# Ten dense blocks, a branch moved ahead, and two tokens per half block in the last layer of a transformer stack

## The chip, the cores and the metric

The program runs on one core of one Trainium2 chip. The metric is its device time in microseconds (us), the median of several runs. One execution is also taken by the hardware profiler, and all rows below come from that one. TensorE is written PE (matmuls) and PEld (weight loads), VectorE DVE, ScalarE ACT, GpSimd POOL, and SyncE, which issues most of the transfers, SP.

## The reference

A stack of two attention layers and a mixer layer over 256 tokens of width 2048 in float32 ends with a feed-forward layer of 16,384 experts, and this last layer is where the change lies. Its weights w_u and w_v have one row of 2048 numbers for each expert. Every token picks 8 x 16 experts through two sets of 128 sub-keys:

```
q  = (h @ w_pq).reshape(T, 8, 2, 128)
s1 = einsum('thd,kd->thk', q[:, :, 0], sub_keys_1);  s2 = the same with q[:, :, 1], sub_keys_2
v1, i1 = top_k(s1, 16);  v2, i2 = top_k(s2, 16)
cand = v1[..., :, None] + v2[..., None, :]           # 16 x 16 for each head
sc, ci = top_k(cand, 16)
e1 = i1[ci // 16];  e2 = i2[ci % 16];  experts = e1 * 128 + e2
gates = softmax(sc)
a = <h_t, w_u[expert]> for each pick;  c = gates * gelu(a)
y_t = sum over picks of c * w_v[expert]
x = rmsnorm(x + y) * g_final
```

## The kernel before, in words

The first 1,530 us are the three layers in front, and the change does not touch them. The rest is the function `peer` (L1283). It does not gather w_u: it multiplies all of it with all tokens, in 128 blocks (one for each e2) of 128 experts (e1), each block in two halves of eight 128 x 128 tiles. Numbers of float32 are split in a hi and a lo part, so one half block is 8 matmuls of hi with the hi and lo parts of the activations (512 columns) and 8 of lo with the hi parts (256 columns). ScalarE makes hi (`wh`, L1464), VectorE lo (`wl`, L1468), two buffers each; the raw weights (`wr`, 512 KB a half block) have four buffers. The result goes through a gelu into the tile C[e1, e2, token].

Beside these half blocks three other things pass, written into them by `between` (L1596), in the written order of PE, ACT and DVE:

- The top-k, on VectorE, as a generator of small steps with weights (`topk_steps`, L1373). Each half block takes steps until their weights sum to 14.
- The picks. When top-k is done (and two short finishing generators), VectorE and ScalarE build one-hot rows for each token (`pair_ops`, L1510), and in the next half block TensorE turns them into the token's gate matrix with four small bfloat16 matmuls (`pair_mms`, L1524). Tokens go by pairs, spread so that the 128th pair is made by half block 194 (`q_end`): most half blocks take two tokens, every sixth or seventh takes four. Every four tokens one multiplication on VectorE (L1537) puts the gates into C.
- When all tokens are through, `places` (L1541) counts which experts are used by the first 128 tokens only, by both halves, by the second only, and by none, and gives each expert row of C a place in that order. `send` (L1580) writes 128 rows of C, 1088 bytes each, to their places in the DRAM tensor `cd`, with one indirect DMA on POOL's queue for each e2. The last ND blocks of e2 are left out: they are dense, all their experts are taken in place from C.

After the w_u blocks comes w_v. `product` (L1658) adds one block's coefficients (256 tokens) times 1024 columns of w_v into eight PSUM banks: 12 matmuls for both token halves, 6 for one. The dense blocks load their w_v rows as they lie (L1706). The others are packed (`packed`, L1726): SP loads 128 packed rows of cd (`cb`, 136 KB), which must wait for all the sends; POOL gathers the 128 w_v rows that they name (`vb`, 1 MB, seven buffers); ScalarE and VectorE split them; TensorE multiplies. `FIRST` and `SECOND` say which packed blocks are multiplied for the first token half and which for the second; blocks behind both are skipped. Should a count overrun these cuts, a flag (`more`, L1572) opens a spare path behind a branch (`tc.If`, L1760) that multiplies what was left out; each engine reads the flag and branches by itself.

Order: in the w_u part PE, ACT and DVE follow the written order. In the w_v part the planner orders all engines by its own model of the time. Instructions on either side of a branch can't be exchanged. The last two packed blocks are fetched and split ahead of the branch and multiplied behind it, bank by bank, with the final norm.

Of the kernel before, what the change touches and what calls it, by code (L numbers as in the profile page):

```python
# [12 lines left out]
BF = mybir.dt.bfloat16  # L13
# [1256 lines left out]
    peer(nc, tc, io, xd1, hT, rbc, hp, sp, W, ident, mm, raw_block, split_block, proj_T, blocks, power_rstd, new_pair)  # L1270


ND = 4
NC = 128 - ND

CROW = 272


FIRST = (0, 76)
SECOND = (26, 103)  # L1280


def peer(nc, tc, io, xd, hT, rbc, hp, sp, W, ident, mm, raw_block, split_block, proj_T, blocks, power_rstd, new_pair):  # L1283
    cd = io["cd"]
    with ExitStack() as es:
# [35 lines left out]
        with ExitStack() as pu_stack:  # L1321
# [185 lines left out]

            bank4 = [None]

            def pair_ops(p):  # L1510

                ws = []
                for t in (2 * p, 2 * p + 1):
                    w = pk.tile([128, 5, 128], BF, name="oh", bufs=4)
                    nc.vector.tensor_scalar(w[:, 4, :], iob, eT[:, 1, t:t + 1], None, op0=OP.is_equal)  # L1515
                    nc.vector.tensor_scalar(w[:, 0, :], iob, eT[:, 0, t:t + 1], None, op0=OP.is_equal)
                    nc.vector.tensor_scalar(w[:, 1, :], iob, eT[:, 1, t:t + 1], gP[:, 0, t:t + 1],
                                            op0=OP.is_equal, op1=OP.mult)
                    for a in (1, 2):
                        nc.scalar.activation(w[:, 1 + a, :], w[:, 4, :], AF.Copy, scale=gP[:, a, t:t + 1])  # L1520
                    ws.append(w)
                return ws

            def pair_mms(p, ws):  # L1524
                if p % 2 == 0:
                    bank4[0] = pq.tile([128, 4, 128], F32, name="pq")
                for i, w in enumerate(ws):
                    t = 2 * p + i
                    for a in range(3):
                        mm(bank4[0][:, t % 4, :], w[:, 0, :], w[:, 1 + a, :], t % 4 == 0 and a == 0, t % 4 == 3 and a == 2)  # L1530
                    mm(cnt[:, t // 128, :], w[:, 0, :], w[:, 4, :], t == 0, t == 255)
                return bank4[0]

            def quad_end(q4, bank, n):
# [54 lines left out]
            steps = topk_steps()  # L1589
            topk_done = False  # L1590
            left = 0
            pair, waiting = 0, []
            placing = q_from = None
            q_end = 2 * 97

            def between(i, low):  # L1596


                nonlocal pair, q4, q_from, left, topk_done, placing
                if not topk_done or fins:  # L1600
                    low()
                    if fins and next(fins[0], "end") == "end":
                        fins.pop(0)
                        if topk_done:

                            nc.vector.tensor_scalar(C[:, :, 256:257].bitcast(I32).rearrange("p a o -> p (a o)"), iob,
                                                    128.0, row, op0=OP.mult, op1=OP.add)
                    left += 14
                    while left > 0 and not topk_done:
                        w = next(steps, None)  # L1610
                        topk_done = w is None
                        left -= w or 0
                    return
                full, ws = [], list(waiting)
                waiting.clear()
                if pair < 128 and q_from is None:
                    q_from = i
                for p, w in ws:
                    b4 = pair_mms(p, w)
                    if p % 2:  # L1620
                        full.append((p // 2, b4))
                while pair < 128 and pair * (q_end - q_from) < 128 * (i + 1 - q_from):
                    waiting.append((pair, pair_ops(pair)))
                    pair += 1
                low()
                if placing and next(placing, "end") == "end":
                    placing = False
                for p, b4 in full:
                    quad_end(p, b4, done[0])
                    q4 += 1  # L1630
                    if q4 == 64:
                        placing = places()
                        next(placing)

            pu_stack.enter_context(tc.manual_schedule(engines={mybir.EngineType.PE, mybir.EngineType.Activation, mybir.EngineType.DVE}))
            split_next(0)()
            for e2 in range(128):
                u_block(e2)
# [19 lines left out]
        def product(c2, b, hi, lo, tbs, first=False, off=0):  # L1658
            for tb in tbs:
                t = slice(tb * 128 - off, (tb + 1) * 128 - off)  # L1660
                for j in range(2):
                    o = py[tb][2 * b + j]
                    w = slice(j * 512, (j + 1) * 512)
                    mm(o, c2[:, 0, t], hi[:, w], first, False)
                    mm(o, c2[:, 1, t], hi[:, w], False, False)
            for tb in tbs:
                t = slice(tb * 128 - off, (tb + 1) * 128 - off)
                for j in range(2):
                    mm(py[tb][2 * b + j], c2[:, 0, t], lo[:, j * 512:(j + 1) * 512], False, False)
# [3 lines left out]
        def split_half(v, b, into=None):  # L1673

            src = v[:, b * 1024:(b + 1) * 1024]
            i = turn[0]
            turn[0] += into is None
            hi = into[0] if into else hp.tile([128, 1024], F32R, name="hT")
            nc.scalar.activation(hi, src, AF.Copy)  # L1679
            if into:  # L1680
                lo = into[1]
            elif i % 3 < 2:
                lo = W["pool"].tile([128, 1024], F32R, name="wr", bufs=W["raw"])
            else:
                lo = W["pool"].tile([128, 1024], F32R, name="wl", bufs=W["lo"])
            nc.vector.tensor_tensor(lo, src, hi.bitcast(F32), op=OP.subtract)  # L1686
            return hi, lo
# [11 lines left out]
        two = []  # L1699

        more_reg = nc.values_load(flag[0:1, 0:1], min_val=0, max_val=1)
        for i, e2 in enumerate(range(NC, 128)):
            c2 = c_place()
            halves(c2, C[:, e2, :256])
            for b in range(2):
                hi, lo = split_block(io["w_v"][e2 * 128:(e2 + 1) * 128, b * 1024:(b + 1) * 1024])  # L1706
                product(c2, b, hi, lo, (0, 1), first=i == 0)
# [5 lines left out]
        def fetch(j, tbs, into=None):  # L1713
            c = vp.tile([128, CROW], F32, name="cb", bufs=8)
            nc.sync.dma_start(c, cd[j * 128:(j + 1) * 128, :])
            v = vp.tile([128, 2048], F32, name="vb", bufs=7)
            nc.gpsimd.indirect_dma_start(v, None, wide, bass.IndirectOffsetOnAxis(c[:, 256:257].bitcast(I32), 0))  # L1717
            c2, off = into or c_place(), 0
            if len(tbs) == 2:
                halves(c2, c[:, :256])  # L1720
            else:
                off = 128 * tbs[0]
                halves(c2[:, :, :128], c[:, off:off + 128])
            return c2, v, off

        def packed(j, tbs):  # L1726
            c2, v, off = fetch(j, tbs)
            for b in range(2):
                hi, lo = split_half(v, b)
                product(c2, b, hi, lo, tbs, off=off)  # L1730
            return v

        def halves_of(j):
            return tuple(tb for tb, (a, z) in enumerate((FIRST, SECOND)) if a <= j < z)

        one = [j for j in range(NC) if len(halves_of(j)) == 1]
        both = [j for j in range(NC) if len(halves_of(j)) == 2]
        last_js, both = both[-2:], both[:-2]
        order, both = both[:4], both[4:]
        late = [xd[:, 0, :], xd[:, 1, :], io["g_final"].to_broadcast([128, D])]  # L1740
        while one or both:
            if one and len(one) >= len(both):
                order.append(one.pop(0))
            else:
                order.append(both.pop(0))
        xg = [vp.tile([128, D], F32, name=f"xg{i}") for i in range(3)]
        for i, j in enumerate(order):
            v = packed(j, halves_of(j))
            if i >= len(order) - 12 and i % 2 == 0 and late:

                k = 3 - len(late)
                nc.gpsimd.tensor_copy(xg[k][:, :1], v[:, :1])
                nc.sync.dma_start(xg[k], late.pop(0))

        last = []
        for i, j in enumerate(last_js):
            c2, v, _ = fetch(j, (0, 1), vp.tile([128, 2, 256], F32R, name="lc", bufs=2))
            last.append((c2, [split_half(v, b, [vp.tile([128, 1024], F32R, name="lw", bufs=8) for _ in range(2)])
                              for b in range(2)]))
        with tc.If(more_reg, preferred_fallthrough_block=False):  # L1760
            for r in range(NC):
                tbs = tuple(tb for tb in range(2) if tb not in halves_of(r))
                if tbs:
                    packed(r, tbs)
        g = xg[2].rearrange("p (c n) -> p c n", c=4)
        rs = []
        for tb in range(2):
# [126 lines left out]
```

## Time and profile before

| | before |
|---|---|
| median of 3 runs | 2858.99 us (2858.84 to 2860.04) |
| the profiled execution | 2855.46 us |
| its span | 2853.7 us |
| PE, PEld busy | 2757.1 us (97%), 2289.3 us (80%) |
| DVE, ACT, POOL busy | 1910.4 us (67%), 1583.8 us (56%), 725.9 us (25%) |
| mean TensorE clock granted | 0.987 of full |

A busy share is an average over stages with different limits, so the table alone does not say what a change in one stage is worth. The page also has the span in forty slices of 71 us:

```
PE   8999999999999999989999999999999993999998
DVE  7545576656767555565566998888887662766665
```

Each digit is the busy share of a slice in tenths, 9 being 90% or more.

### The profile page before, as it was taken

Reading aid. Unit: us, or ns where it says so; the run is one execution under the profiler, and the core shown is the slowest. Engines: PE = TensorE matmul, PEld = TensorE weight load, DVE = VectorE, ACT = ScalarE, POOL = GpSimd, SP = SyncE. Lnnn points to the kernel's source line nnn. Section 1 sums busy time; section 2 is a strip of 40 time slices with the busy share of each in tenths; the row PEclk is TensorE's granted clock in tenths of the full one; section 3 lists DMA queues with packets and bytes.
Section 4 is the critical chain, followed back from the end, with each engine's and each line's share of the span. In section 5 each row is a group of like instructions: output and inputs, shape, how many; then the busy total and the mean of one; then the engine's idle time right before and its main releaser. Section 6 shows DMA issues by size and latency. Waiting matters only on the chain. (4 is left out here: it accounts for less than half of the span.)

```text
span 2853.7 us, 41401 instructions
## 1 busy us (share of the span) xinstructions
PE 2757.1 (97%) x14566; PEld 2289.3 (80%) x14566; DVE 1910.4 (67%) x3525; ACT 1583.8 (56%) x2943; POOL 725.9 (25%) x669
## 2 busy tenths in 40 slices
PE   8999999999999999989999999999999993999998
PEld 5877778887788888878888888888888882888886
DVE  7545576656767555565566998888887662766665
ACT  4445565545565544444454455888775442655554
POOL 6312320103121000020001232212223885322330
PEclk9999999999999999999999999999999996999999
DMA  6566443665445655566565555444445885988883
GB/s 229 174 220 196 135 141 119 208 191 172 155 129 163 229 199 167 180 214 224 167 202 178 181 186 182 147 149 147 148 145 178 265 263 226 343 290 298 282 323 126
DMA packets 158810, 561.74 MB, mean 197 GB/s; under 512 B 19584, under 2 KB 33536, under 8 KB 145024
## 3 DMA queue, kind: packets, MB, share of 16 engines
q1 hardware_dynamic: 137808, 433.71, 47.4%
q0 software_dynamic: 20784, 125.29, 11.7%
q8 instruction: 117, 1.92, 0.3%
q14 instruction: 101, 0.83, 0.1%
HBM read 531.17 MB, written 27.75 MB: 196 GB/s over the span
## 5 line engine op out<-in xcount | busy, mean ns | idle before, releaser
L204 DVE TENSOR_TENSOR wl<-wr,wh 128x1024 fp32r<-128x1024 f32 (+1 forms) x467 | 598.7, 1284 | 469.8 <-ACT wh L202 399.3
L202 ACT ACTIVATE wh<-wr 128x1024 fp32r<-128x1024 f32 (+1 forms) x467 | 492.9, 1056 | 588.6 <-PE pp L187 500.4
L187 PE MATMUL pp<-hT,wh 128*128 128x512 f32 x2880 | 736.8, 398 | 0.0
L187 PE MATMUL pp<-wh,hT 128*128 128x512 f32 x2688 | 697.0, 400 | 5.6 <-ACT wh L202 3.7
L187 PEld LDWEIGHTS pp<-wh,hT 128*128 128x128 f32 x2688 | 502.2, 190 | 128.6 <-ACT wh L202 8.5
L187 PEld LDWEIGHTS pp<-hT,wh 128*128 128x128 f32 x2880 | 517.1, 189 | 94.4 <-issue 0.3
L187 PEld LDWEIGHTS pp<-hT,wl 128*128 128x128 f32 x2880 | 393.0, 190 | 29.3 <-DVE wl L204 0.7
L187 PE MATMUL pp<-hT,wl 128*128 128x256 f32 x2880 | 403.0, 283 | 0.3 <-DVE wl L204 0.3
L187 PE MATMUL pp<-wl,hT 128*128 128x512 f32 x1344 | 373.9, 400 | 10.7 <-DVE wl L204 10.7
L1468 DVE TENSOR_TENSOR wl<-wr,wh 128x1024 fp32r<-128x1024 f32 x256 | 315.1, 1231 | 19.7 <-ACT wh L1464 17.7
L187 PEld LDWEIGHTS pp<-wl,hT 128*128 128x128 f32 x1344 | 248.3, 189 | 68.9 <-DVE wl L204 13.8
L1464 ACT ACTIVATE wh<-wr 128x1024 fp32r<-128x1024 f32 x256 | 269.9, 1054 | 39.8 <-PE pp L187 23.3
L1679 ACT ACTIVATE hT<-vb 128x1024 fp32r<-128x1024 f32 x202 | 210.8, 1059 | 127.9 <-PE py L187 98.1
L1686 DVE TENSOR_TENSOR wr<-vb,hT 128x1024 fp32r<-128x1024 f32 x135 | 165.4, 1229 | 66.8 <-PE py L187 53.5
L1717 POOL DMA_INDIRECT vb<-w_v,cb x103 | 127.2, 1234 | 269.0 <-ACT hT L1679 97.4
L1584 POOL DMA_INDIRECT cd<-C,posi x124 | 168.1, 1356 | 50.4 <-issue 31.7
L1520 ACT ACTIVATE oh<-oh,gP 128x128 bf16<-128x128 bf16 x512 | 166.8, 391 | 20.1 <-DVE oh L1515 19.8
L187 PE MATMUL py<-hT,c 128*128 128x512 f32 x600 | 152.6, 389 | 0.0
L187 PE MATMUL py<-hT 128*128 128x512 f32 x592 | 150.4, 389 | 0.0
L187 PEld LDWEIGHTS py<-hT,c 128*128 128x128 f32 x600 | 112.6, 188 | 23.3
L187 PEld LDWEIGHTS py<-hT 128*128 128x128 f32 x592 | 111.1, 188 | 23.0
L1686 DVE TENSOR_TENSOR wl<-vb,hT 128x1024 fp32r<-128x1024 f32 x67 | 82.2, 1228 | 33.5 <-PE py L187 27.1
(444 smaller groups left out, 3055.7 us busy)
## 6 DMA issues: line engine op xcount, KB each, us to landing
wr<-w_u SPq DMA_DIRECT2D x256, 512.0 KB
wr<-w_even SPq DMA_DIRECT2D x104, 512.0 KB
wr<-w_out SPq DMA_DIRECT2D x96, 512.0 KB
wr<-w_odd SPq DMA_DIRECT2D x96, 512.0 KB
wr<-w_in SPq DMA_DIRECT2D x64, 512.0 KB
wr<-w_mem SPq DMA_DIRECT2D x32, 512.0 KB
wr<-w_pq SPq DMA_DIRECT2D x32, 512.0 KB
cb<-cd SPq DMA_DIRECT2D x103, 136.0 KB
```

Source lines behind the costliest of these rows:

```text
L187: nc.tensor.matmul(out, lhsT=lhsT, rhs=rhs, start=start, stop=stop, skip_group_check=True)
L202: nc.scalar.activation(hi, raw, AF.Copy)
L204: (lo_eng or nc.vector).tensor_tensor(lo, raw, hi.bitcast(F32), op=OP.subtract)
L1464: nc.scalar.activation(hi, raw, AF.Copy)
L1468: nc.vector.tensor_tensor(lo, raw, hi.bitcast(F32), op=OP.subtract)
L1520: nc.scalar.activation(w[:, 1 + a, :], w[:, 4, :], AF.Copy, scale=gP[:, a, t:t + 1])
L1584: i = nc.gpsimd.indirect_dma_start(cd, bass.IndirectOffsetOnAxis(posi[:, e2:e2 + 1], 0), src, None).ins
L1679: nc.scalar.activation(hi, src, AF.Copy)
L1686: nc.vector.tensor_tensor(lo, src, hi.bitcast(F32), op=OP.subtract)
L1717: nc.gpsimd.indirect_dma_start(v, None, wide, bass.IndirectOffsetOnAxis(c[:, 256:257].bitcast(I32), 0))
```

## The change

Ten blocks are dense instead of four, so 118 instead of 124 are sent and packed, and the cuts follow. Top-k steps are taken by 16 units instead of 14. From the half block in which the picks begin, each takes exactly two tokens. The dense blocks and the fetch and split of the first two packed blocks (both token halves) stand in a region in which PE, ACT, DVE and SP follow the written order. Behind it stands the branch, and behind the branch the products of these two blocks and all other packed blocks. The last two blocks are fetched in the same way as before, without a branch behind them.

```diff
-ND = 4
+ND = 10
 NC = 128 - ND
-FIRST = (0, 76)
-SECOND = (26, 103)
+FIRST = (0, 73)
+SECOND = (25, 99)
...
-            def pair_ops(p):
-                ws = []
-                for t in (2 * p, 2 * p + 1):
-                    w = pk.tile([128, 5, 128], BF, name="oh", bufs=4)
...
+            def token_ops(t):
+                w = pk.tile([128, 5, 128], BF, name="oh", bufs=4)
...
-            q_end = 2 * 97
...
-                    left += 14
+                    left += 16
...
-                while pair < 128 and pair * (q_end - q_from) < 128 * (i + 1 - q_from):
-                    waiting.append((pair, pair_ops(pair)))
-                    pair += 1
+                while tok < min(256, 2 * (i + 1 - q_from)):
+                    waiting.append((tok, token_ops(tok)))
+                    tok += 1
...
         more_reg = nc.values_load(flag[0:1, 0:1], min_val=0, max_val=1)
+        e = mybir.EngineType
+        head = ExitStack()
+        head.enter_context(tc.manual_schedule(engines={e.PE, e.Activation, e.DVE, e.SP}))
         for i, e2 in enumerate(range(NC, 128)):
...
-        last_js, both = both[-2:], both[:-2]
-        order, both = both[:4], both[4:]
+        first_js, order, last_js, both = both[:2], both[2:4], both[-2:], both[4:-2]
...
-        for i, j in enumerate(order):
-            v = packed(j, halves_of(j))
...
-        last = []
-        for i, j in enumerate(last_js):
-            c2, v, _ = fetch(j, (0, 1), vp.tile([128, 2, 256], F32R, name="lc", bufs=2))
-            last.append((c2, [split_half(v, b, [vp.tile([128, 1024], F32R, name="lw", bufs=8) for _ in range(2)])
-                              for b in range(2)]))
+        def ahead(js):
+            out = []
+            for j in js:
+                c2, v, _ = fetch(j, (0, 1), vp.tile([128, 2, 256], F32R, name="lc", bufs=2))
+                out.append((c2, [split_half(v, b, [vp.tile([128, 1024], F32R, name="lw", bufs=8) for _ in range(2)])
+                                 for b in range(2)]))
+            return out
+        first = ahead(first_js)
+        head.close()
         with tc.If(more_reg, preferred_fallthrough_block=False):
             for r in range(NC):
                 tbs = tuple(tb for tb in range(2) if tb not in halves_of(r))
                 if tbs:
                     packed(r, tbs)
+        for c2, ws in first:
+            for b in range(2):
+                product(c2, b, *ws[b], (0, 1))
+        for i, j in enumerate(order):
+            v = packed(j, halves_of(j))
...
+        last = ahead(last_js)
         g = xg[2].rearrange("p (c n) -> p c n", c=4)
```

## Rows read from the trace of the kernel before

**Rows 1.** Windows: stretch, length, busy us of each engine, clock, DMA share, GB/s

```profile
1534.40:1754.30 219.90, 219.90 (x1279) 194.12 (x1278) 206.68 (x582) 114.03 (x164) 63.88 (x70) 1.00 0.56 184
...
2189.00:2352.50 163.50, 163.50 (x940) 143.98 (x939) 108.04 (x151) 80.51 (x120) 135.77 (x92) 1.00 0.89 266
...
2363.40:2408.20 44.80, 0.00 (x0) 0.00 (x0) 0.43 (x1) 2.44 (x4) 29.50 (x31) 0.55 0.43 155
2408.20:2425.50 17.30, 16.27 (x62) 12.98 (x63) 12.81 (x13) 10.83 (x13) 3.41 (x3) 0.89 1.02 411
2425.50:2827.80 402.30, 402.28 (x1775) 332.88 (x1773) 268.25 (x299) 233.38 (x297) 119.50 (x97) 1.00 0.80 290
```

**Rows 2.** Timeline of PE at the turn: start, us, instructions [idle before, releaser]

```profile
2408.23 3.78 PE L187 MATMUL py<-wh,hT 128*128 128x512 f32 x8 [44.86 <-ACT wh L202]
```

**Rows 3.** Timeline of SP's queue from 2340 to 2405 us

```profile
2340.69 13.59 SPq L195 DMA_DIRECT2D wr<-w_v  x6
2398.17 2.99 SPq L1715 DMA_DIRECT2D cb<-cd  x8
2401.26 1.24 SPq L195 DMA_DIRECT2D wr<-w_v  x2
```

**Rows 4.** Waits of PE from 2340 us on: us in total, times, longest

```profile
PE py L187 <- issue: 4.0, 1, 4.0
```

**Rows 5.** Timeline of PE, two half blocks of w_u without tokens

```profile
2251.74 2.00 PE L187 MATMUL pp<-hT,wh 128*128 128x512 f32 x8
...
2254.53 2.00 PE L187 MATMUL pp<-hT,wh 128*128 128x512 f32 x8
```

**Rows 6.** Groups of DVE, 1534 to 1754 us: busy us, mean ns | idle before

```profile
L1468 DVE TENSOR_TENSOR wl<-wr,wh 128x1024 fp32r<-128x1024 f32 x77 | 96.0, 1247 | 6.8 <-ACT wh L1464 6.7
```

**Rows 7.** Groups of DVE, 1776 to 2172 us

```profile
L1468 DVE TENSOR_TENSOR wl<-wr,wh 128x1024 fp32r<-128x1024 f32 x110 | 133.9, 1217 | 7.8 <-ACT wh L1464 7.8
```

**Rows 8.** Timeline of PE, hi matmuls of half blocks that take tokens

```profile
1893.15 2.09 PE L187 MATMUL pp<-hT,wh 128*128 128x512 f32 x8
...
1909.92 2.08 PE L187 MATMUL pp<-hT,wh 128*128 128x512 f32 x8
...
1913.23 2.08 PE L187 MATMUL pp<-hT,wh 128*128 128x512 f32 x8
...
1917.74 2.09 PE L187 MATMUL pp<-hT,wh 128*128 128x512 f32 x8
```

**Rows 9.** Groups of POOL, 2189 to 2352 us

```profile
L1584 POOL DMA_INDIRECT cd<-C,posi x91 | 135.6, 1490 | 40.4 <-issue 27.1 <-DVE more L1574 13.0 <-DMA cd<-C,posi 0.3
```

**Rows 10.** Timeline of POOL, 2300 to 2307 us

```profile
2300.42 1.90 POOL L1584 DMA_INDIRECT cd<-C,posi  x1 [0.30 <-issue]
...
2306.01 1.89 POOL L1584 DMA_INDIRECT cd<-C,posi  x1 [0.30 <-issue]
```

**Rows 11.** Timeline of DVE beside it

```profile
2300.26 1.22 DVE L1468 TENSOR_TENSOR wl<-wr,wh 128x1024 fp32r<-128x1024 f32 x1
```

**Rows 12.** Timeline of POOL, 2352 to 2400 us

```profile
2352.26 0.96 POOL L1584 DMA_INDIRECT cd<-C,posi  x1 [0.30 <-issue]
...
2359.41 0.96 POOL L1584 DMA_INDIRECT cd<-C,posi  x1 [0.30 <-issue]
...
2393.56 0.96 POOL L1584 DMA_INDIRECT cd<-C,posi  x1 [0.30 <-issue]
2399.19 0.99 POOL L1717 DMA_INDIRECT vb<-w_v,cb  x1 [4.67 <-issue]
```

**Rows 13.** Timeline of ACT, first conversion of a gathered block

```profile
2406.17 1.06 ACT L1679 ACTIVATE hT<-vb 128x1024 fp32r<-128x1024 f32 x1 [7.36 <-DMA vb<-w_v,cb]
```

**Rows 14.** The branch's line, L1760: ns min/median/max, first to last start

```profile
L1760 POOLq EVENT_SEMAPHORE  x4: 17/43/5298, 2797.9 to 2803.4; - x4
L1760 SPq COMPARE_BRANCH  x2: 43/48/53, 2787.4 to 2792.4; - x2
...
L1760 PEldq COMPARE_BRANCH  x2: 90/1912/3733, 2824.2 to 2828.0; - x2
```

More of the change, by code (lines that the diff above doesn't have):

```diff
@@ L1508, in peer, with token_mms @@
             bank4 = [None]
-            def pair_ops(p):
-                ws = []
-                for t in (2 * p, 2 * p + 1):
-                    w = pk.tile([128, 5, 128], BF, name="oh", bufs=4)
[L1515 to L1525, printed above, removed]
-                    bank4[0] = pq.tile([128, 4, 128], F32, name="pq")
[L1527 to L1531, printed above, removed]
+            def token_ops(t):
+                w = pk.tile([128, 5, 128], BF, name="oh", bufs=4)
+                nc.vector.tensor_scalar(w[:, 4, :], iob, eT[:, 1, t:t + 1], None, op0=OP.is_equal)
+                nc.vector.tensor_scalar(w[:, 0, :], iob, eT[:, 0, t:t + 1], None, op0=OP.is_equal)
+                nc.vector.tensor_scalar(w[:, 1, :], iob, eT[:, 1, t:t + 1], gP[:, 0, t:t + 1],
+                                        op0=OP.is_equal, op1=OP.mult)
+                for a in (1, 2):
+                    nc.scalar.activation(w[:, 1 + a, :], w[:, 4, :], AF.Copy, scale=gP[:, a, t:t + 1])
+                return w
+            def token_mms(t, w):
+                if t % 4 == 0:
+                    bank4[0] = pq.tile([128, 4, 128], F32, name="pq")
+                for a in range(3):
+                    mm(bank4[0][:, t % 4, :], w[:, 0, :], w[:, 1 + a, :], t % 4 == 0 and a == 0, t % 4 == 3 and a == 2)
+                mm(cnt[:, t // 128, :], w[:, 0, :], w[:, 4, :], t == 0, t == 255)
                 return bank4[0]
@@ L1591, in peer @@
             left = 0
-            pair, waiting = 0, []
+            tok, waiting = 0, []
             placing = q_from = None
-            q_end = 2 * 97
             def between(i, low):
-                nonlocal pair, q4, q_from, left, topk_done, placing
+                nonlocal tok, q4, q_from, left, topk_done, placing
                 if not topk_done or fins:
@@ L1615, in between @@
                 waiting.clear()
-                if pair < 128 and q_from is None:
+                if q_from is None:
                     q_from = i
[L1618 to L1621, printed above, removed]
-                while pair < 128 and pair * (q_end - q_from) < 128 * (i + 1 - q_from):
-                    waiting.append((pair, pair_ops(pair)))
-                    pair += 1
+                for t, w in ws:
+                    b4 = token_mms(t, w)
+                    if t % 4 == 3:
+                        full.append((t // 4, b4))
+                while tok < min(256, 2 * (i + 1 - q_from)):
+                    waiting.append((tok, token_ops(tok)))
+                    tok += 1
                 low()
@@ L1633, in between @@
                         next(placing)
-            pu_stack.enter_context(tc.manual_schedule(engines={mybir.EngineType.PE, mybir.EngineType.Activation, mybir.EngineType.DVE}))
+            e = mybir.EngineType
+            pu_stack.enter_context(tc.manual_schedule(engines={e.PE, e.Activation, e.DVE}))
             split_next(0)()
@@ L1701, in peer @@
         more_reg = nc.values_load(flag[0:1, 0:1], min_val=0, max_val=1)
+        e = mybir.EngineType
+        head = ExitStack()
+        head.enter_context(tc.manual_schedule(engines={e.PE, e.Activation, e.DVE, e.SP}))
         for i, e2 in enumerate(range(NC, 128)):
@@ L1746, in peer @@
         xg = [vp.tile([128, D], F32, name=f"xg{i}") for i in range(3)]
+        def ahead(js):
[7 more added lines that the diff above has]
+        head.close()
+        with tc.If(more_reg, preferred_fallthrough_block=False):
+            for r in range(NC):
+                tbs = tuple(tb for tb in range(2) if tb not in halves_of(r))
+                if tbs:
+                    packed(r, tbs)
+        for c2, ws in first:
+            for b in range(2):
+                product(c2, b, *ws[b], (0, 1))
         for i, j in enumerate(order):
@@ L1753, in peer @@
                 nc.sync.dma_start(xg[k], late.pop(0))
-        last = []
-        for i, j in enumerate(last_js):
-            c2, v, _ = fetch(j, (0, 1), vp.tile([128, 2, 256], F32R, name="lc", bufs=2))
-            last.append((c2, [split_half(v, b, [vp.tile([128, 1024], F32R, name="lw", bufs=8) for _ in range(2)])
-                              for b in range(2)]))
[L1760 to L1764, printed above, removed]
+        last = ahead(last_js)
         g = xg[2].rearrange("p (c n) -> p c n", c=4)
```

## Prediction

> **What bounds the kernel now.** I read the page's forty slices first: PE stands at 8 or 9 tenths in all but the 34th, where it falls to 3. So TensorE sets the time, and the question is where it waits and how much it is given. Next the windows by stage [rows 1]. The reader is to see that TensorE is busy without a gap while the w_u blocks pass (from 1534 to 2352 us, but for the token work, below) and again from 2425.5 to 2827.8, and that it does nothing from 2363.4 to 2408.2. That is the turn from w_u to w_v: two of the four dense blocks run, then TensorE stands 44.86 us [rows 2]. The queue of SP says why the other two did not fill it: six dense loads, then the cb loads (which wait until the last send has landed), and only then the last two dense loads, at 2401.26 [rows 3]. The second place is near the end: 4.0 us before the last 48 matmuls, put down to issue [rows 4]; it is the branch at L1760. Of VectorE the reader is to see 206.68 of 219.9 us in the top-k stage [rows 1]: it is almost the bound there.
>
> **The change, part by part.** Units first. A half block of w_u without tokens takes 2.79 us (8 hi matmuls at 2251.74, the next 8 at 2254.53) [rows 5]. A w_v matmul takes 402.28 / 1775 = 0.2266 us [rows 1], so 12 of them, one dense half block, 2.72 us. I call the end of TensorE's w_u work T; it is 2352.5 now.
>
> *Top-k at 16 units a half block, not 14.* The weights that the generator yields sum to 1064: done in half block 66 instead of 76, the first token in 73 instead of 83. It comes earlier but denser. VectorE had 206.7 us over 77 half blocks: 96.0 for wl [rows 6], so 111 for top-k and the little that goes with each block. In 67 half blocks: 83.5 + 111 = 194 at most. TensorE needs 67 x 2.79 + 4.8 (what 219.9 has over 77 x 2.79, the score matmuls) = 192. They are level, so what VectorE can't avoid idling is lost: of its 13.2 idle us now, 6.8 lie ahead of wl (they go when it is late itself). I take +5; bounds 0 (all of it hidden by the buffers) and +13 (all idle stays).
>
> *Two tokens in each of 128 half blocks.* Now 256 tokens go into 110 half blocks and a few, two tokens in most and four in every sixth or seventh; 110 wl in the 396 us from 1776 to 2172 [rows 7] are 3.60 each. After a four-token one, half blocks of two run at (1913.23 - 1893.15) / 6 = 3.35 us in a row of six, and the four-token one that follows takes 4.51 [rows 8]. Four tokens cost the hi and lo halves of the next steps their time on ACT and VectorE, and two do not. The same tokens now: 111 x 3.60 + 17 x 2.79 = 447 for 128 half blocks. Changed: 128 x 3.37 = 431, so -16; I take -13, since 3.37 rests on one run. Bounds: -23 (3.31, as from 1909.92 to 1913.23) and +10 (3.57, nearly as now). TensorE's w_u stage in all: -8.
>
> *The sends.* The last token comes in half block 200, not 193, so the first send comes 7 half blocks nearer to T: 7 x 2.79 = 19.5 us. 91 sends fit before T now [rows 9]; three take 5.59 us there (2300.42 to 2306.01) [rows 10], so about 80 fit, and 118 - 80 = 38 are left, against 33 now. Their pace then decides. A send that begins inside a VectorE instruction is stretched: that of 2300.42 took 1.90 us [rows 10], with VectorE's wl from 2300.26 for 1.22 us [rows 11], where one alone takes 0.96, with 0.30 ahead of it [rows 12]. In the dense stage wl comes once in 2.72 us, evenly, instead of twice in 5.59 unevenly. Bounds: 1.27 a send, as with no VectorE work, and 1.86 as before T (29 in the dense stage, the other 9 at 1.27). I take 1.45, nearest to the dense part of now (2352.26 to 2359.41, five sends, 1.43 each) [rows 12]: the last begins at T + 55 (bounds 48 and 65).
>
> *Ten dense blocks in written order.* 20 half blocks x 2.72 = 54.4 us that need no send, so they end at T + 54.4. The data must come at 512 KB in 2.72 us, 193 GB/s, and the sends add 139 KB in 1.45 us, 96 GB/s: 289 in all, against 266 at a DMA share of 0.89 before T and 290 at 0.80 in the packed stage [rows 1]. I count no delay for it. From the last send (2393.56) to the first gather is 5.6 us [rows 12], to its first conversion 12.6, and that takes 1.06 [rows 13]: 13.7. With two gathers instead of seven side by side I take 13. Packed work begins at T + 68, and TensorE idles 13.6 us instead of 44.8: -31 (bounds -39 and -20).
>
> *More matmuls.* A dense block takes 24, a packed block 24 or 12. Now: 96 + 50 x 24 + 53 x 12 = 1932. Changed: 240 + 48 x 24 + 51 x 12 = 2004. 72 x 0.2266 = +16.3. The tighter cuts do not open the spare path: by the reference's own picks the rows of one half only are 3366 (25 blocks need 3200), those up to the end of both 9001 (73 blocks hold 9344), all used ones 12320 (99 hold 12672).
>
> *The branch moved ahead.* At the end it costs TensorE 4.0 us, 3733 ns of it the branch instruction that jumps; the one that falls through takes 90 [rows 14]. That goes: -4. At the new place TensorE's jump lies in its 13.6 us of waiting. What is late next is the third packed block, for SP and POOL pass the branch too, and everything behind it in their queues (the cb loads and gathers of all later blocks) waits. SP's two branches stand 5.0 us apart, and POOL waited 5.3 us there for gathers to land [rows 14]. Counted from the last send: SP has issued both cb at 6 (the first at 4.6 now [rows 3]), its second branch is at 11, with a jump like TensorE's its third cb load at 15; POOL's third gather at 17, landed 7 later, converted at 25. TensorE, from 13 on, has 48 matmuls, 10.9 us, and 2 more because the first eight after an idle stretch took 3.78 us instead of 8 x 0.2266 [rows 2]: until 26. It is just covered; I take +1, bounds 0 and +6. The slow start itself stands now too (17.3 us for 62 matmuls worth 14.0, at a granted clock of 0.89) [rows 1]: 0.
>
> [...]
>
> Written order for PE, ACT, DVE and SP by itself I cost at nothing: the order is what the parts above rest on.
>
> **Sum.** -8 - 31 + 16 - 4 + 1 = -26, from the profiled execution's 2855.46 to 2829.5. The median of the runs, 2858.99, is 3.5 above that execution, so 2833.
>
> **Rivals.**
> *The sends stay at 1.86.* For: VectorE also converts here. Against: an even rhythm, and 1.43 in the dense part now. The last begins at T + 65, packed work at T + 78.7, the gap is 24.3: -20 in place of -31, -15 in all, 2844.
> *The token work saves nothing.* For: VectorE and ACT work as much per token. Against: the six steps in a row at 3.35. At 3.57 the w_u stage takes +15 instead of -8, so 2856.
> *The branch restarts the gathers too slowly.* For: two jumps on SP, and the drain on POOL. Against: two whole blocks of TensorE work are ahead of it. With +6 for the third block and as much for the next ones: 2844.
> *All goes well.* 3.31 a half block, top-k hidden, two sends in each dense half block (1.36, the last at T + 52): -23 - 35 + 16 - 4 = -46, 2813. Against: it needs three bounds at once.
> *VectorE is the bound of all three, and it is slower.* Top-k +13, half blocks with tokens at 3.57 (+10), sends held at 1.86: +23 - 20 + 16 - 4 + 1 = +16, 2875. It decides if VectorE falls behind at 16 units, that is, if 194 us of work can't be packed closer than the 94% of now. For: the level sum above. Against: the run at 3.35.
> *The dense blocks don't fill the gap.* If a dense load still stands behind a cb load on SP [rows 3], two blocks run, the sends end at T + 48, packed work starts at T + 61 with 1956 matmuls left, 443 us: T + 507 with the slow start, against T + 490 now by the same terms (438 + 44.8 + 4.0 + 3.3); with -8 that is 2868. Against: the region orders SP as written, dense loads first. This is also the case in which the change does not do what it says.
>
> **Chances.** Forecast 2833 (its own range 2823 to 2841): 0.42. All well: 0.15. Slow sends: 0.17. Slow restart: 0.09. Tokens save nothing: 0.08. VectorE bound: 0.06. Dense blocks don't fill: 0.03. About 0.2%, 5.7 us, is what a measurement here can tell from no change. The first four are faster, and a third of the fifth: 0.86. Half of the fifth lies within: 0.05 with the edge. Slower 0.09. The range 2810 to 2856 leaves out the last two cases, half of the fifth and an edge of the best.
>
> **What would show it.** TensorE's idle stretch at the turn: 14 us (25: slow sends; 45: not filled). The first send some 144 us ahead of T; the send's mean in the dense stage. Half blocks of w_u with tokens at 3.37, those with top-k at 2.79 but for the scores. No issue wait of 4 us ahead of the last 48 matmuls. A wait of TensorE for the third block's conversion of under 2 us. The forecast is wrong if w_u does not end earlier, or if TensorE waits after the branch for more than one block.

## The result, and the profile after

The changed kernel takes 2831.4 us (median of 4 runs, 2831.0 to 2835.5), the kernel before 2859.5 beside it: a ratio of 0.9907, interval 0.9896 to 0.9919. Forecast: 2833. The profiled execution took 2830.97 us, 24.5 less than that of before; the sum had said 26 less. T is again the end of TensorE's w_u work: 2339.7, 12.6 earlier.

| term (us) | forecast | measured |
|---|---|---|
| w_u: top-k at 16 units | +5 | +5.7 |
| w_u: two tokens per half block | -13 | -17.1 |
| rest of w_u, and the layers in front | 0 | -1.1 |
| TensorE's waits between T and packed work | -31 | -33.3 |
| 72 more matmuls (1932 to 2004, as counted; 0.2267 us each) | +16.3 | +16.3 |
| slow clock and short waits, third block with them | +1 | +4.8 |
| branch away from the end | -4 | -4.0 |
| closing of the program | 0 | +4.2 |

Windows of the changed kernel, by the same stages as [rows 1], the turn cut finer (stretch, length, busy us of PE, PEld, DVE, ACT, POOL, clock, DMA share, GB/s):

```profile
1534.40:1753.40 219.00, 216.29 (x1245) 187.34 (x1244) 204.16 (x587) 114.58 (x163) 65.60 (x69) 1.00 0.54 178
1753.40:2183.60 430.20, 428.83 (x3076) 376.23 (x3074) 378.87 (x1028) 345.87 (x894) 76.56 (x126) 1.00 0.47 156
2183.60:2339.70 156.10, 155.24 (x902) 136.46 (x900) 104.64 (x154) 75.72 (x114) 121.86 (x80) 1.00 0.86 256
2339.70:2408.65 68.95, 61.35 (x242) 47.41 (x240) 27.77 (x32) 23.51 (x32) 46.72 (x42) 0.90 0.71 235
2408.65:2413.59 4.94, 0.00 (x0) 0.00 (x0) 3.50 (x4) 3.70 (x5) 0.00 (x0) 0.99 0.36 148
2413.59:2426.60 13.01, 12.74 (x48) 10.09 (x48) 2.33 (x5) 1.97 (x5) 5.79 (x6) 0.87 0.72 229
2426.60:2815.90 389.30, 389.29 (x1716) 322.00 (x1716) 266.00 (x302) 231.05 (x302) 113.82 (x96) 1.00 0.80 297
```

The second row is the token stage, 128 half blocks in 430.2 us (the sum had 431), TensorE busy in 428.83 of them. In the fourth, the dense blocks, 240 matmuls worth 54.4 us take 68.95: 7.6 idle, and 7.0 more at a mean granted clock of 0.90. The idle pieces are called holes below. TensorE's idle stretch of 44.86 us [rows 2] is gone; its timeline at the turn, the waits in brackets, and ScalarE's conversion ahead of the longest hole:

```profile
2348.68 2.11 PE L187 MATMUL py<-wh,c 128*128 128x512 f32 x8 [0.62 <-issue]
...
2352.93 2.14 PE L187 MATMUL py<-wh,hT 128*128 128x512 f32 x8 [1.24 <-ACT wh L202]
...
2384.08 1.98 PE L187 MATMUL py<-wh,hT 128*128 128x512 f32 x8
...
2388.95 3.23 PE L187 MATMUL py<-wh,c 128*128 128x512 f32 x8 [1.99 <-issue]
...
2397.44 3.78 PE L187 MATMUL py<-wh,c 128*128 128x512 f32 x8 [2.65 <-issue]
...
2413.59 12.74 PE L187 MATMUL py<-lw,lc 128*128 128x512 f32 x48 [4.95 <-ACT lw L1674]
2426.61 2.12 PE L187 MATMUL py<-hT,c 128*128 128x512 f32 x8 [0.28 <-ACT hT L1674]
```

```profile
2396.34 1.06 ACT L202 ACTIVATE wh<-wr 128x1024 fp32r<-128x1024 f32 x1 [7.44 <-remote]
```

SP's queue, where two dense loads used to stand behind eight cb loads [rows 3], now has all twenty first, and among the cb loads a pause, from the second at 2399.9 to the third at 2415.29:

```profile
2328.06 57.83 SPq L195 DMA_DIRECT2D wr<-w_v  x20
2399.49 20.22 SPq L1714 DMA_DIRECT2D cb<-cd  x10
```

The same queue from 2414 us on, where the cb loads behind the branch begin:

```profile
2415.29 4.42 SPq L1714 DMA_DIRECT2D cb<-cd  x8
```

What the queue did in the pause: its own two branch instructions, and its waits from 2395 to 2420 us (us in total, times, longest; the wait of 9.8 ends at 2412.2, the one of 3.0 at 2415.2):

```profile
L1757 SPq COMPARE_BRANCH  x2: 38/48/57, 2400.3 to 2402.4; - x2
```

```profile
SPq L1714 <- DMA vb<-w_v,cb: 15.5, 2, 9.8
SPq L1714 <- DVEq L1757: 3.0, 1, 3.0
```

POOL's sends before T and in the dense stage ([rows 9] before), and the branch's line, whose jump stood at the end in [rows 14] (ns min/median/max, first to last start):

```profile
L1579 POOL DMA_INDIRECT cd<-C,posi x79 | 120.7, 1527 | 32.9 <-issue 23.8 <-DVE more L1569 9.1
```

```profile
L1579 POOL DMA_INDIRECT cd<-C,posi x40 | 45.4, 1135 | 12.2 <-issue 11.9 <-DMA cd<-C,posi 0.3
```

```profile
L1757 PEldq COMPARE_BRANCH  x2: 90/2394/4697, 2405.0 to 2408.8; - x2
```

The last send begins at 2395.07, T + 55.4 (forecast T + 55), the first at T - 144.4 (forecast 144), 1.45 us apart on average in the dense stage, as taken. The jump begins at 2408.84, right behind the last dense matmul, and ends at 2413.54; packed work follows at once, though its first half was converted by 2409.2. The row names ACT because its semaphore came last among those that the profile shows; the jump is the cause.

### The profile page after: what moved, and what is told of

The parts are those of the page before. It is cut to its first block, busy times and chain, and to the rows that moved or that the text cites. A ratio compares the mean times of both kernels' runs of the same rounds, so it can differ in the third digit from the quotient of the medians.

```text
span 2829.2 us, 41674 instructions
## 1 busy us (share of the span) xinstructions
PE 2770.2 (98%) x14638; PEld 2300.1 (81%) x14638; DVE 1915.9 (68%) x3524; ACT 1589.5 (56%) x2957; POOL 710.0 (25%) x670
## 5 line engine op out<-in xcount | busy, mean ns | idle before, releaser
L204 DVE TENSOR_TENSOR wl<-wr,wh 128x1024 fp32r<-128x1024 f32 (+1 forms) x479 | 614.1, 1284 | 494.2 <-ACT wh L202 396.7
L202 ACT ACTIVATE wh<-wr 128x1024 fp32r<-128x1024 f32 (+1 forms) x479 | 505.8, 1056 | 623.5 <-PE pp L187 498.3
L187 PEld LDWEIGHTS pp<-hT,wl 128*128 128x128 f32 x2880 | 391.3, 190 | 35.5 <-DVE wl L1468 7.6
L1674 ACT ACTIVATE hT<-vb 128x1024 fp32r<-128x1024 f32 x190 | 197.0, 1057 | 104.1 <-PE py L187 75.6
L1681 DVE TENSOR_TENSOR wr<-vb,hT 128x1024 fp32r<-128x1024 f32 x126 | 153.9, 1226 | 57.5 <-PE py L187 41.2
L1716 POOL DMA_INDIRECT vb<-w_v,cb x99 | 119.4, 1206 | 247.9 <-ACT hT L1674 76.5
L187 PE MATMUL py<-hT,c 128*128 128x512 f32 x568 | 144.2, 389 | 0.3 <-ACT hT L1674 0.3
L187 PE MATMUL py<-hT 128*128 128x512 f32 x544 | 138.3, 389 | 0.0
L187 PEld LDWEIGHTS py<-hT,c 128*128 128x128 f32 x568 | 106.5, 188 | 22.8 <-ACT hT L1674 0.7
L187 PEld LDWEIGHTS py<-hT 128*128 128x128 f32 x544 | 102.1, 188 | 21.2
L1681 DVE TENSOR_TENSOR wl<-vb,hT 128x1024 fp32r<-128x1024 f32 x64 | 78.6, 1228 | 33.3 <-PE py L187 20.6
```

What stands on the lines that cost most here:

```text
L187: nc.tensor.matmul(out, lhsT=lhsT, rhs=rhs, start=start, stop=stop, skip_group_check=True)
L202: nc.scalar.activation(hi, raw, AF.Copy)
L204: (lo_eng or nc.vector).tensor_tensor(lo, raw, hi.bitcast(F32), op=OP.subtract)
```

## The experiments

Ratios are to the kernel before on the same chip and carry 95% intervals; the changed kernel's is 0.9907. "+10 us" is the difference of ratios times 2858.

**Fourteen units.**

```diff
-                    left += 16
+                    left += 14
```

> Only the top-k units are undone: 14 a half block again, the rest as in the changed kernel (2831.4 us). Theory (the sum's terms, at their measured sizes): the top-k half blocks lose their 5.7 us of waiting, but the first token comes in half block 83 instead of 73, so the first send is 10 half blocks (28 us, 15 sends) nearer to the end of w_u, the last send begins about 20 us later after it, and packed work begins at T + 90 instead of T + 74: -6 + 16 = +10, 2841 us. Rival (the units matter only for the top-k stage, the sends are hidden by the dense blocks): -6, 2825.5 us.

Measured: 2850.0 us, 0.9993 (0.9978 to 1.0008): +25; its twelve times spread from 2848 to 2866. The profiled execution is 19.2 longer, where +10 was expected: T 3.6 earlier, the last send at T + 77.4, packed work at T + 89.6 instead of T + 73.9, and 7.1 more behind that.

```profile
2425.73 13.99 PE L187 MATMUL py<-lw,lc 128*128 128x512 f32 x48 [34.65 <-ACT lw L1674]
2443.36 2.92 PE L187 MATMUL py<-hT,c 128*128 128x512 f32 x6 [3.64 <-ACT hT L1674]
```

The first wait is the forecast one. The second, for the third block, was not in the sum and is read below. The units are worth more through the sends than they cost in top-k.

**Token pairs again.** `pair_ops` and `pair_mms` as before, `q_end` 184 for 111 half blocks from half block 73.

> Only the pace of the tokens is undone: pairs again, 256 tokens in 111 half blocks with four in every sixth or seventh, from the same first half block 73. Theory: the half blocks with tokens take 447 us over 128 half blocks instead of 430, +17; but the first send comes 16 half blocks (45 us, 24 sends) further ahead of T, so the last one begins near T + 24 and is no longer what packed work waits for; what it waits for then is the end of the dense blocks. If the 14 us that the dense stage takes too long come from the sends beside it, that stage is 54 us long and packed work begins near T + 60: +17 - 14 = +3, 2834 us. Rival (the dense stage is long by itself, with its two buffers of wh and wl, sends or not): +17, 2848 us.

Measured: 2833.4 us, 0.9914 (0.9901 to 0.9926): +2. T at 2355.6, 15.9 later; the last send at T + 15.3; the dense blocks end at T + 54.6 without a hole; packed work at T + 58.4. Tokens that are through in 111 half blocks instead of 128 cost w_u 15.9 us and let the sends end 40 us earlier against T. At the end that bought nothing, because ten dense blocks and the jump became the bound:

```profile
2414.05 12.80 PE L187 MATMUL py<-lw,lc 128*128 128x512 f32 x48 [3.83 <-issue]
```

**The branch at the end.** The `tc.If` block moved back behind `last = ahead(last_js)`.

> Only the branch is undone: it stands behind the fetch of the last two blocks again. The prediction's term: +4 at the end, nothing at the turn, 2835.4 us. Theory after seeing the trace: the jump is not hidden at the turn either, since the dense blocks end at T + 69 and TensorE starts packed work the moment its 4.7 us jump is over, while the first conversion was there 4.4 us earlier; so the turn gains 4.4 what the end loses: within 1 us of 2831.4.

Measured: 2839.5 us, 0.9941 (0.9928 to 0.9954): +10; the profiled execution +5.2. A miss for the second theory, and above the prediction's 4.

```profile
2340.20:2395.30 55.10, 55.10 (x242) 44.74 (x240) 27.49 (x31) 22.76 (x30) 43.82 (x38) 1.00 0.77 251
2395.30:2412.40 17.10, 0.01 (x1) 0.00 (x0) 1.59 (x5) 2.66 (x6) 9.34 (x10) 0.62 0.66 225
2412.40:2435.00 22.60, 22.60 (x91) 18.49 (x92) 16.11 (x17) 13.13 (x16) 6.35 (x6) 0.91 1.02 419
```

These are the dense blocks, the gap and the first packed work; the two rows below are the last 48 matmuls, here and in the changed kernel. The same dense blocks, loads and sends run here in 55.1 us without a hole, as forecast, and yet packed work begins at T + 72.2, only 1.7 sooner: the holes of the changed kernel were paid out of the gap. No jump is in this gap, but the first gather took 8.2 us to its conversion (2403.1 to 2411.3) with six others beside it, against 5.7 (2402.5 to 2408.2) where the branch lets only two go. So the moved branch costs the turn almost nothing, and the jump's 3.8 at the end is saved, with the slow clock behind it: after that wait the last 48 matmuls run at a granted clock of 0.82 and take 2.6 us longer than in the changed kernel. The profiled 5.2 is these 2.6 and 3.8, T 0.5 later, and the 1.7.

```profile
2807.47 13.66 PE L187 MATMUL py<-lw,lc 128*128 128x512 f32 x48 [3.79 <-issue]
```

```profile
2804.85 11.09 PE L187 MATMUL py<-lw,lc 128*128 128x512 f32 x48
```

**Four dense blocks.** `ND = 4`, `FIRST = (0, 76)`, `SECOND = (26, 103)`.

> Only the number of dense blocks is undone: 4 of them and the old cuts, with the new order, branch, units and token pace. Theory: the dense stage ends at T + 22 (no hole in it), six more sends end 8 us later, packed work begins near T + 78 instead of T + 74 with the jump inside the wait, and has 72 more matmuls, 16.3 us: +20, 2851 us. Rival (the order and the dense stage's waits cost what its blocks bring): the changed kernel's time within 5 us, 2826 to 2836.

Measured: 2849.5 us, 0.9972 (0.9961 to 0.9984): +19. The dense blocks end at T + 22.5, the last send comes at T + 60.2 and packed work at T + 73.8, as with ten and 4 sooner than expected; what is left is the matmuls, and a third block that is late:

```profile
2414.11 12.55 PE L187 MATMUL py<-lw,lc 128*128 128x512 f32 x48 [51.26 <-ACT lw L1674]
2431.84 3.78 PE L187 MATMUL py<-hT 128*128 128x512 f32 x8 [5.18 <-ACT hT L1674]
```

**Two dense loads.**

```diff
+        raws = []
...
-                hi, lo = split_block(io["w_v"][...])
+                if i == 0:
+                    raws.append(raw_block(io["w_v"][...]))
+                hi = W["pool"].tile([128, 1024], F32R, name="wh", bufs=W["hi"])
+                nc.scalar.activation(hi, raws[b], AF.Copy)
...
```

> The changed kernel with only the first two dense loads; the other 18 half blocks are split from the same two tiles, so 18 loads are left out and the rest of the work stays. In the changed kernel TensorE's semaphore increments reached ScalarE and VectorE up to 10 us late while sends ran beside dense loads. Theory (sends and loads together are too much): no increment later than 1 us, the dense blocks end at T + 54.4. Rival (the sends alone do it): increments 3 to 10 us late as before. The end of the last send stays the bound either way: packed work between T + 66 and T + 74.

This kernel leaves out 18 loads of w_v, so most of its products are of the wrong rows; only its times are read. Measured: 2831.2 us (one run). The rival holds in one half: the holes are there without the loads. That the sends alone make them is not shown. TensorE, then ScalarE:

```profile
2382.79 1.98 PE L187 MATMUL py<-wh,c 128*128 128x512 f32 x8
...
2394.74 3.78 PE L187 MATMUL py<-wh,c 128*128 128x512 f32 x8 [3.56 <-issue]
```

```profile
2393.63 1.06 ACT L1709 ACTIVATE wh<-wr 128x1024 fp32r<-128x1024 f32 x1 [7.14 <-remote]
```

The conversion of 2393.63 waits for the buffer that the matmuls of 2382.79 read; they ended at 2384.77, and the release came 8.9 us later. In the changed kernel the conversion at 2396.34 waited in the same way for matmuls that ended at 2386.06. Where no send ran beside them (the kernels with three and four tokens below), the dense blocks ended at T + 21.9 for four, no hole; beside sends, the profiled executions of some kernels have holes (the changed one, this, the next, the one with six blocks) and of others none (the branch at the end, and four blocks, T + 22.5). So the holes need not come with every send, and what sets them off is open.

**A short jump.**

```diff
-            for r in range(NC):
+            for r in range(NC - 1, NC):
                 tbs = tuple(tb for tb in range(2) if tb not in halves_of(r))
```

> The changed kernel with the spare path cut to one block, so that the jump over it is short (the path is not entered with this data, and the results need no more of it). Theory (the jump is long because it goes far, and the instructions behind it have to be fetched): TensorE's second branch takes under 0.5 us instead of 4.7, and packed work begins with the first conversion: 0 to 4 us are gained, 2827 to 2831. Rival (any jump of TensorE drains and refills its queue): 3.5 to 4.7 us as before, and no gain.

Measured: 2828.6 us, 0.9906 (0.9891 to 0.9921): no gain that can be told. The short jump comes as the theory had it, the gain does not; that a long one has instructions to fetch is not shown:

```profile
L1757 PEldq COMPARE_BRANCH  x2: 85/135/185, 2400.4 to 2404.0; - x2
```

```profile
2408.47 13.88 PE L187 MATMUL py<-lw,lc 128*128 128x512 f32 x48 [4.67 <-ACT lw L1674]
```

The jump takes 0.185 us (4.697 in the changed kernel), and TensorE waits for the conversion instead, at 2407.4: seven gathers are issued here before the first has landed, and that one takes 8.0 us from its issue to its conversion. SP's third cb load stands at 2397.7. In the changed kernel it came at 2415.29, 0.1 behind VectorE's split of the second block; the same 0.1 is there in the kernels with 14 units, with pairs and with four dense blocks. With the long path SP is through its own branch instructions at 2402.4, and its third load then waits 9.8 us, to 2412.2, for the landing of the two gathers and 3.0 more for a semaphore that VectorE gives at the branch, behind its last split. With the short one it waits for neither.

**Without the region.**

```diff
-        head.enter_context(tc.manual_schedule(engines={e.PE, e.Activation, e.DVE, e.SP}))
```

> Only the region is undone: the planner orders the dense blocks and the first packed ones, the branch stays behind them. By its order of SP's queue 18 of the 20 dense loads stand ahead of the two cb loads and two behind. Theory: nine dense blocks end at T + 49, the tenth comes behind the last send, inside the wait for the first gather: packed work begins no later than 5 us after the changed kernel's, 2831 to 2836 us. Rival (without the written order the dense blocks don't fill the gap): an idle stretch of over 30 us as before, 2850 us or more.

Measured: 2840.7 us, 0.9947 (0.9933 to 0.9960): +11, over twice the most that was expected.

```profile
2400.45 0.79 ACT L1650 ACTIVATE lc<-cb 128x256 fp32r<-128x256 f32 x2 [22.44 <-SPq L1756]
```

```profile
2402.23 3.76 PE L187 MATMUL py<-wh,c 128*128 128x512 f32 x8 [18.98 <-ACT wh L202]
```

Not SP's order but ScalarE's: the planner put the conversion of the first cb ahead of the last four dense halves, and that waits for the last send. Two dense blocks end up behind the gap, and packed work begins at T + 82.2.

**Four tokens, three tokens.** `min(256, 4 * (i + 1 - q_from))`, then 3, both with four dense blocks.

> Four tokens in each half block instead of two, and four dense blocks with their old cuts: what if the sends could be over by T? The tokens are through 64 half blocks earlier, some 180 us, so all sends but those of the last blocks are out before T. Theory: a token costs TensorE 0.365 us at that pace (in the kernel before, half blocks with four took 1.46 more than those without) instead of 0.285, so T comes 20 us later; but the last send begins near T - 15, packed work follows the four dense blocks and the jump at T + 26 instead of T + 74, with 72 more matmuls, 16 us, and 5 of refill: +20 - 48 + 21 = -7, 2824 us. Rival (four in every half block keep ScalarE and VectorE from the next half block, 4.5 us each with two buffers of one-hot rows): T 36 us later, 2840 us.

> Three tokens in every half block (86 of them) and four dense blocks with their old cuts. With four tokens T came 52 us later, 4.70 us a half block. Theory: three take 3.8 us, T comes 14 us later than with two, the sends are over by T as they were with four, packed work begins at T + 26: 2353.7 + 26.3 + 420.5 and 13 to the end, 2815 us. Rival (three in a row wear out the buffers as four did, 4.2 us each): T 48 us later than with two, 2849 us.

Measured: 2849.9 us, 0.9976 (0.9967 to 0.9985), and 2830.9 us, 0.9902 (0.9885 to 0.9918). The sends were over 12.6 us ahead of T in both, and packed work began at T + 26.3 and T + 26.8, as expected. The price of the tokens was missed: 64 half blocks of 4.70 us (T 51.8 later) and 85 of 4.02 (T 34 later). The token stages:

```profile
1754.30:2055.20 300.90, 287.20 (x2051) 229.07 (x2050) 266.30 (x931) 259.03 (x733) 58.59 (x63) 1.00 0.32 111
```

```profile
1755.80:2100.90 345.10, 335.47 (x2403) 281.19 (x2402) 303.87 (x965) 288.98 (x789) 64.82 (x84) 1.00 0.39 131
```

With two tokens a half block took 3.31 us at the median, 0.52 over 2.79. At 0.26 a token four would take 64 x 3.83 = 245 us of the 300.9 here, and three 85 x 3.57 = 303 of the 345.1. The rest is 56 and 42 us. In it TensorE's weight loads, which come ahead of each token's matmuls, stand idle (four tokens, three, and two in the changed kernel: us in total, times, longest):

```profile
PEld L187 <- issue: 35.9, 185, 0.2
```

```profile
PEld L187 <- issue: 22.4, 114, 0.3
```

```profile
PEld L187 <- issue: 3.5, 18, 0.3
```

That they wait for one-hot rows, which VectorE makes (busy 0.88 in all three stages) and ScalarE (0.86 and 0.84, against 0.80), is the likely reading; the rows name no releaser, so it is not shown.

**Pairs with six and five dense blocks, and tokens spread singly.** `ND = 6`, cuts (0, 75) and (26, 102), with the pairs above; the same with `256 * (i + 1 - q_from) // 112` single tokens; and five dense blocks.

> The changed kernel with the old token pairs (as in the experiment with pairs, 111 half blocks) and six dense blocks (cuts 0 to 75 and 26 to 102). Theory: with pairs the sends are over at T + 15, and what packed work waits for is the dense blocks and the jump behind them, so four dense blocks fewer pay: they end at T + 33, four more sends at T + 21, packed work begins at T + 36.5 instead of T + 58.4, and has 48 more matmuls, 10.9 us: 11 us less than with ten, 2822 us. Rival (the gathers can't start sooner; packed work begins no sooner than T + 48): no gain over ten, 2833 us.

> As the experiment with pairs and six dense blocks, but with the 256 tokens spread singly over 112 half blocks: two in most, three in every third or fourth, four in none. Theory (what is dear in the old pace is four at once: 17 half blocks at 4.24 us and what they take from the next ones): three tokens take 3.8 us, T comes 5 us later than with two in each of 128, not 16, and all else is as with pairs: 2812 us. Rival (a token costs VectorE and ScalarE the same however they are spread): T as with pairs, 2822 us.

> Pairs again, five dense blocks instead of six (cuts 0 to 75 and 26 to 102). With six, TensorE ended them at T + 35.5 and began packed work at T + 40.2, after the jump; the first conversion of a gathered block came at T + 35.3. Theory: with five the dense blocks and the jump end at T + 32 to 35, one more send puts the last at T + 21.5 and the first conversion at T + 34 to 36: both bounds meet, packed work begins near T + 36 and has 12 more matmuls, 2.7 us: 0 to 2 us less than with six, 2821 us. Rival (the waits of the dense stage stay with the sends, whatever its length): packed work near T + 38.5, and nothing gained, 2823 to 2825 us.

Measured: 2822.7 us, 0.9879 (0.9862 to 0.9895); 2824.4 us, 0.9887 (0.9870 to 0.9903); 2824.6 us, 0.9886 (0.9869 to 0.9902). Six dense blocks with pairs are the best version, 8 us below the changed kernel (the intervals just part); the other two can't be told from it. Some 4 of the 8 are the closing, read below. Packed work began at T + 40.2 (the dense blocks had holes again and ended at T + 35.5), T + 39.4 and T + 35.2. Spreading the tokens did not help: three cost 3.76 us as thought, but the two-token half blocks among them took 3.50 instead of 3.36: 400.5 us for 112, and pairs took 399.6 to 399.8 for 111. With five, TensorE starts 5 us sooner and then waits for the third block:

```profile
2389.58 12.82 PE L187 MATMUL py<-lw,lc 128*128 128x512 f32 x48 [7.55 <-ACT lw L1680]
2407.21 3.24 PE L187 MATMUL py<-hT 128*128 128x512 f32 x7 [4.81 <-ACT hT L1680]
```

## Why the prediction was right, and where its steps were not

*Top-k* (+5): +5.7, read from half-block periods of TensorE: the 73 up to the first token take 12.0 us more than 2.79 each, the 83 in the kernel before took 6.3 more. *Tokens*: the row of six steps in [rows 8] stood for all: 3.36 on average over 128. (The sum used 3.37 where that row gives 3.35, without a reason; the average lies between.) The -16 worked out from it was right, and taking only -13 was not needed. Other slips in the sums (219.9 is 5.1 over 77 x 2.79, not 4.8; a bound of -38 for the gap, not -39, and -34 in the best case, not -35) move nothing by more than 1 us.

*Sends and the gap* (-31): the last send and its pace came out as taken, and the first conversion was done 14.1 us behind the last send (forecast 13). The step that failed is the one that ended the dense blocks at T + 54.4 and put TensorE's jump inside a wait of 13.6. With the holes they ended at T + 69, the jump came behind the last dense matmul, and 4.4 of its 4.7 stand between the first conversion and packed work, which began at T + 74 instead of T + 68. The idle time is still as forecast, since the holes and the jump lie in what would have been the wait.

*The branch moved* (-4 and +1): the 4.0 went, and with it 1.8 that the sum did not have. Behind that wait the last 48 matmuls took 12.91 us at a granted clock of 0.87; without it they take 11.09 at 1.00, in the row shown above.

```profile
2831.76 12.91 PE L187 MATMUL py<-lw,lc 128*128 128x512 f32 x48 [3.98 <-issue]
```

The step on the restart was right that the wait for the gathers' landing would hold it up, and wrong in the rest. SP made no jump like TensorE's: its two branch instructions take 0.04 and 0.06 us and are over 7.3 us behind the last send (forecast 11 for the second, 15 for the end of the jump). The gathers' landing holds the third cb load until 17.1, and VectorE's splits, which the sum did not have, until 20.2 (forecast 15); its block is converted at 31.5 (25). TensorE's own delay covered it: 0.28 us of waiting. That is why the late jump cost so little, by this estimate: had TensorE begun at 2409.2, its 48 matmuls (12.74) would have ended at 2421.9, and it would have waited for the third block until the same 2426.6, as it does with 14 units (3.64), four dense blocks (5.18) and five (4.81). The rival "the branch restarts the gathers too slowly" had the right place; in this kernel its price is hidden, and with an earlier start it is not.

*Slow clock* (0): the dense stage lost 7.0 us, 5.6 of it in the 24 matmuls between 2388.95 and 2403, behind its holes, where the granted clock was 0.52 (eight took 3.78 us at 2397.44, at 0.50), and the start of packed work 1.9, against 2.3 before (the 3.3 of [rows 1], less a wait of 1.0); the 1.8 at the end came back. *Closing* (0): a term that the sum did not have. POOL's last drain takes 9.77 us, before 1.93 (drain lines of the changed kernel, then of the kernel before):

```profile
L1892 POOLq DRAIN  x3: 45/113/9773, 2818.6 to 2828.9; - x3
```

```profile
L1883 POOLq DRAIN  x3: 45/113/1933, 2847.3 to 2853.4; - x3
```

The program ends 4.2 us later behind its last product. Every kernel here with ten dense blocks closes 13.2 to 13.6 us after its last product, those with four to six 9.0 to 9.4, whatever else they change. The number of dense blocks sets that of POOL's transfers (217 sends and gathers against 224 to 227), and no run tells the two apart; why either should count is open.

So 2833 was met in part by luck, by terms that cancel: w_u gave 4.5 more than its -8, the waits 2 more than their -31, and the clock and the closing took back 8. Nor did the median lie 3.5 above the profiled execution, as the last step took over from the kernel before; it lay 0.4 above, and the sum for that execution was 1.5 too low. What the decomposition hangs on was shown singly: the number of dense blocks (19 us), the written order (11), the branch's place (5 to 10), the units (19 to 25) and the token pace (2).

## What to carry to other kernels

A gap in front of a bound is a reserve: what is moved into it is free until the sum of it reaches the bound, so count the holes, the jump and the restart together and not each against the whole gap. When a step is made earlier, name what was late just behind it; here three things, the dense blocks, the jump and the third gather, stood within 5 us of one another, and taking one away showed the next. Work that fills a gap should be reduced again once the gap is shortened: six dense blocks, with the tokens through in 111 half blocks, beat ten at either token pace.

## What the runs showed of the hardware

Beside or just behind back-to-back sends, TensorE's semaphore releases reached ScalarE and VectorE late, as far as the trace tells: by up to 10.3 us in the changed kernel, and by 8.9 without the loads. Kernels with sends and no hole stand beside these, so the sends are not shown to be the cause. In the changed kernel the trace has fewer landing events in the same stage: 31 beside 197 packets of 4 bytes between 2340 and 2350 us, against 117 beside 125 between 2310 and 2320; but with pairs, where no hole is, it has 41 beside 188 between 2360 and 2370. Whether this has to do with the late releases, no run shows. It stays open.

Of the changed kernel's sends, the 67 that began inside a TENSOR_TENSOR of VectorE took 1.73 us on average, and the 50 that began beside no VectorE instruction took 0.96.

TensorE's jump took 3.4 to 6.8 us over a long path (13 profiles; 4.70 in the changed kernel, 3.73 in the kernel before), 0.185 over a short one, and in every profile it started 0.2 us behind the last matmul ahead of it, so none of it ran beside that work.
